# MLP up-projection in seven block products, two pairs interleaved, and the down-projection behind it

## The chip, the cores and the metric

The kernel runs on one core of one Trainium2 chip. The metric is the device time of one execution in microseconds (us). The core has five instruction streams that run beside each other: TensorE (PE, matmuls; its weight loads are listed as PEld), VectorE (DVE), ScalarE (ACT), GpSimd (POOL) and SyncE (SP, which only issues DMAs here). They wait for each other through semaphores.

## The reference, cut to what matters

One encoder layer over 1024 tokens of width 1024. The change concerns the second sub-layer, the gated MLP (`D_FF` = 2816 = 22 x 128), and the output projection `w_o` just ahead of it:

```python
y = _token_mixer(h, ...)          # ends in the product with w_o
x = x + gt1 * _rmsnorm(y, norm_w[l, 1])
h = _rmsnorm(x, norm_w[l, 2]) * (1.0 + sc2) + sh2
...
hu = _dwconv(h @ w_up, conv_w, FFN_CONV // 2) + conv_b     # 1024 -> 5632, width-3 conv over tokens
a, b = jnp.split(hu, 2, axis=-1)
y = (jax.nn.silu(a) * b) @ w_down                           # 2816 -> 1024
x = x + gt2 * _rmsnorm(y, norm_w[l, 3])
```

## The kernel before

Every large product is made three times over: each float32 operand is split by `split` (L166 and L169) into a high part, rounded by ACT, and a low part, the difference, made by DVE or POOL; `mm3` then issues high x high, high x low and low x high into one PSUM bank. One such matmul is 128x512 (128 rows of output, 512 columns).

The last third of the kernel has three stages. (1) `wo_tile(t)` (L1403 on), once for each of eight blocks of 128 tokens: 48 matmuls `y<-wo,mg` into two PSUM banks, k = 0 to 6 of both halves first and k = 7 of both behind, since the merged operand `mg` is ready last for k = 7; then squares on ACT, a power on POOL, scaling and the residual on DVE, and a second norm that leaves `x1[t]`. `h2_half` (L1438) transposes `x1` on PE (`x1T`, eight groups of four), scales it (`hf`) and splits it into `h`. (2) The up-projection, `up_mm`: 44 blocks of 128 rows of `w_up`, each 2 halves x 8 k x 3 = 48 matmuls `hu`, in all 2112. `up` reads the PSUM tile (L1509 on ACT, L1510 and L1511 on DVE: the conv over tokens); `pair(f)` takes block f and block 22+f, applies Silu, multiplies (L1520) and splits the product into `gh`, `gl` in SBUF. (3) The down-projection `down(c)`: two f at a time, 8 token blocks x 2 halves x 2 f x 3 = 96 matmuls `yp`, whose PSUM result DVE adds into `yac` (L1552); in all 1056 matmuls. Stages 2 and 3 alternate: after four pairs, one `down` and two pairs, nine times; `last_down` takes the last four f and ends in the norm and the output.

The weights come by DMA from SP: 512 KB a block (`wur<-w_up`, `wdr<-w_dn`). PSUM has eight banks of 512 columns: `hu` has two tiles of two banks, `yp` four of one bank. The order of instructions on each engine is fixed when the kernel is built, by a scheduler that starts from program order and the dependencies; `T.kept = True` keeps PE's in program order, and the wrapper `InOrder(tc, V)` does so for another engine.

Of the kernel before, what the change touches and what calls it, by code (L numbers as in the profile page):

```python
# [1604 lines left out]
```

## Time and profile before

| | us |
|---|---|
| median of 3 runs | 2046.57 (2046.24 to 2051.73) |
| profiled execution, its own time | 2046.33 |
| span of that execution in the trace | 2044.5 |
| PE busy | 1987.2 (97% of the span) |
| DVE busy | 1198.8 (59%) |
| ACT busy | 776.7 (38%) |
| POOL busy | 318.8 (16%) |
| mean granted PE clock | 0.993 of full speed |

The busy time of PE is read with care: matmuls are pipelined, so the record of one (some 390 ns) overlaps the next. What counts is the spacing from start to start. The chain of waits gives it: a piece of the chain lists a duration and a count of matmuls that ran without waiting. The rows of all views stand in the section of rows, ahead of the prediction.

### The profile page before, as it was taken

How to read it: one execution, taken by the hardware profiler on the slowest of the kernel's cores; microseconds unless marked ns; L12 is line 12 of the kernel's file. 1: busy time of each engine (PE TensorE's matmuls, PEld its weight loads, DVE VectorE, ACT ScalarE, POOL GpSimd, SP SyncE). 2: the span in 40 equal slices, each digit the busy share in tenths (PEclk: the TensorE clock that was granted, in tenths of full speed). 3: DMA queues.
4: the chain of work that ended last, by engine and by line, in shares of the span. 5: the costliest groups of instructions: out<-in, count | busy, mean ns of one | idle time of the engine just before them, and what ended most of it. 6: DMA issues, size and time to landing. Idle time of an engine off the chain costs nothing. (4 is left out here: it accounts for less than half of the span.)

```text
span 2044.5 us, 27253 instructions
## 1 busy us (share of the span) xinstructions
PE 1987.2 (97%) x10846; PEld 1661.5 (81%) x10846; DVE 1198.8 (59%) x2033; ACT 776.7 (38%) x1320; POOL 318.8 (16%) x291
## 2 busy tenths in 40 slices
PE   7999999999999998989999999999999999999998
PEld 6978887888888887768888878878888888888886
DVE  7367867476666658674578653552534454444437
ACT  6464543353353232553555442433221222221222
POOL 4321121141041110133000041010110001000101
PEclk9999999999999999999999999999999999999999
DMA  8321121132121076545201153121111111111113
GB/s 293 114 73 62 43 73 58 47 104 70 34 98 63 31 253 204 162 145 162 90 11 41 43 185 109 69 73 52 42 52 52 52 32 61 52 41 45 48 51 135
DMA packets 68178, 175.09 MB, mean 86 GB/s; under 512 B 10257, under 2 KB 17745, under 8 KB 68050
## 3 DMA queue, kind: packets, MB, share of 16 engines
q1 hardware_dynamic: 54658, 143.13, 22.4%
q10 hardware_dynamic: 11088, 21.83, 2.8%
q0 software_dynamic: 2304, 8.39, 1.0%
q8 instruction: 85, 1.39, 0.3%
q14 instruction: 43, 0.35, 0.1%
HBM read 143.07 MB, written 30.24 MB: 85 GB/s over the span
## 5 line engine op out<-in xcount | busy, mean ns | idle before, releaser
L128 PE MATMUL hu<-h,wuh 128*128 128x512 f32 x1408 | 434.2, 390 | 1.6 <-DVE cv L1511 1.6
L128 PEld LDWEIGHTS hu<-h,wuh 128*128 128x128 f32 x1408 | 263.8, 188 | 56.5 <-ACT cv L1509 2.0
L128 PE MATMUL pj<-hhi,wth 128*128 128x512 f32 x704 | 293.8, 417 | 7.0 <-ACT vN L906 5.4
L128 PE MATMUL pj<-hhi,wtl 128*128 128x512 f32 x704 | 277.3, 394 | 0.0
L128 PE MATMUL pj<-hlo,wth 128*128 128x512 f32 x704 | 275.9, 392 | 0.0
L128 PE MATMUL hu<-h,wul 128*128 128x512 f32 x704 | 274.0, 389 | 0.0
L169 DVE TENSOR_TENSOR wul<-wur,wuh 128x512 fp32r<-128x512 f32 x44 | 30.5, 692 | 215.1 <-ACT wuh L166 215.1
L128 PEld LDWEIGHTS pj<-hhi,wth 128*128 128x128 f32 x704 | 133.5, 190 | 27.9 <-ACT vN L906 5.9
L128 PEld LDWEIGHTS pj<-hhi,wtl 128*128 128x128 f32 x704 | 132.7, 189 | 28.7
L128 PEld LDWEIGHTS hu<-h,wul 128*128 128x128 f32 x704 | 132.2, 188 | 27.5
L169 POOL TENSOR_TENSOR wul<-wur,wuh 128x512 fp32r<-128x512 f32 x44 | 57.6, 1310 | 612.3 <-ACT wuh L166 535.9
L128 PEld LDWEIGHTS pj<-hlo,wth 128*128 128x128 f32 x704 | 133.7, 190 | 20.1
L128 PE MATMUL yp<-wdh,gh 128*128 128x512 f32 x336 | 132.7, 395 | 0.0
L128 PE MATMUL yp<-wdh,gl 128*128 128x512 f32 x336 | 132.7, 395 | 0.0
L128 PE MATMUL yp<-wdl,gh 128*128 128x512 f32 x336 | 132.6, 395 | 0.0
L169 POOL TENSOR_TENSOR wtl<-wtr,wth 128x512 fp32r<-128x512 f32 x44 | 62.3, 1415 | 409.2 <-ACT wth L166 324.3
L166 ACT CAST wuh<-wur 128x512 fp32r<-128x512 f32 x88 | 53.9, 614 | 188.6 <-PE hu L128 188.6
L1552 DVE TENSOR_TENSOR yac<-yac,yp 128x512 f32<-128x512 f32 x128 | 87.1, 686 | 53.5 <-PE yp L128 53.0
L128 PE MATMUL y<-wo,mg 128*128 128x512 f32 x384 | 88.9, 391 | 0.0
L166 ACT CAST wth<-wtr 128x512 fp32r<-128x512 f32 x88 | 53.3, 617 | 83.4 <-PE pj L128 56.2
L128 PEld LDWEIGHTS y<-wo,mg 128*128 128x128 f32 x384 | 71.6, 188 | 15.1 <-DVE mg L169 0.4
L166 ACT CAST wdh<-wdr 128x1024 fp32r<-128x1024 f32 x21 | 22.0, 1049 | 159.4 <-PE yp L128 110.5
(442 smaller groups left out, 4088.7 us busy)
## 6 DMA issues: line engine op xcount, KB each, us to landing
wtr<-w_t SPq DMA_DIRECT2D x44, 512.0 KB, 3.5
wur<-w_up SPq DMA_DIRECT2D x44, 512.0 KB, 3.6
adaw<-w_adaT SPq DMA_DIRECT2D x64, 256.0 KB, 4.0
...
g<-gt_d SPq DMA_DIRECT2D x24, 512.0 KB, 4.3
wdr<-w_dn SPq DMA_DIRECT2D x22, 512.0 KB, 3.6
ada_w<-w_adaT SPq DMA_DIRECT2D x16, 512.0 KB, 5.5
...
```

Source lines behind the costliest of these rows:

```text
L128: self.queue(self.nc.tensor.matmul(out, w, x, **kw), x, 4 if x.dtype == F32 else 1)
L166: ins = A.copy(hi, src)
L169: (eng or V).tensor_tensor(lo, src, r32(hi), op=ALU.subtract)
L1552: V.tensor_tensor(yac[t][:, sl], yac[t][:, sl], ps, op=ALU.add)
```

## The change

**Up-projection.** The 2x2 block form of the product (output rows: block p and block 22+p; inner dimension: k = 0 to 3 and k = 4 to 7; tokens: first and second 512) is computed with seven products of 128x512 over four k, in place of eight. One product is `prod`: 4 k x 3 = 12 matmuls. The products of a pair are `m1` to `m7`; `uA` and `uB` are two PSUM tiles of two banks for each of two pairs in flight, all eight banks. Between products ACT copies a bank (`A.copy` in `m1`, `m7_copy`) and DVE adds a bank and a copy (`e_add`, and the add in `m5`). The operand sums over tokens are built once, in `F` (`t13`, `t2`, `t4`) and split (`hi` on ACT, `lo` on DVE or POOL) into `B11`, `B21`, `T1` to `T4`, `B22`; the weight sums are built for every pair, by DVE (`sums_32`) and POOL (`sums_14`). For the first two pairs `m7` and `m6` are made in two column parts, 384 and 128, since the last 128 tokens come late; `m1` of these two pairs has one matmul more, which starts the second bank.

**Gated product.** `gated` writes `silu(a) * b` to DRAM (`g_d`, 512 KB a pair) instead of splitting it. **Down-projection.** It comes behind all pairs: for each of two groups of 512 tokens (`gr`), 22 f in turn are loaded (`wdr`, 512 KB, and `gr`, 256 KB), split, and multiplied into all eight banks at once, three matmuls to a bank; the last four f go bank by bank. The count stays 2 x 22 x 8 x 3 = 1056. The adds into `yac` are gone.

**Output projection.** `wo_mm` runs all eight k of half 0, then of half 1. `h2_tile` transposes each token block behind the next block's matmuls instead of four blocks at a time. `big` holds 8 tiles of [128, 4, 512] instead of 32 of [128, 512].

```diff
+    def big_tile(nm):
+        return big.tile([P, 4, 512], F32R, tag="big", name=nm, bufs=8)
...
-        xt = tp.tile([P, D], F32, tag="xt", name="xt", bufs=2)
-        SY.dma_start(xt, I["x"][tk, :])
-        x1[t] = x1p.tile([P, D], F32, tag="x1", name="x1", bufs=6)
-        pss = [ps_mm.tile([P, 512], F32, tag="mm", name="y") for _ in range(2)]
-        for ks in (range(KT - 1), (KT - 1,)):
-            for hf in range(2):
-                sl = slice(hf * 512, hf * 512 + 512)
-                for k in ks:
-                    mm3(pss[hf], mg[hf_][0][k][:, c_], mg[hf_][1][k][:, c_], wo[k][0][:, sl], wo[k][1][:, sl], k == 0, k == KT - 1)
+        xts[t] = tp.tile([P, D], F32, tag="xt", name="xt")
+        SY.dma_start(xts[t], I["x"][t * P : (t + 1) * P, :])
+        wo_ps[t] = [ps_mm.tile([P, 512], F32, tag="mm", name="y") for _ in range(2)]
+        for hf in range(2):
+            sl = slice(hf * 512, hf * 512 + 512)
+            for k in range(KT):
+                mm3(wo_ps[t][hf], mg[hf_][0][k][:, c_], mg[hf_][1][k][:, c_], wo[k][0][:, sl], wo[k][1][:, sl], k == 0, k == KT - 1)
...
+    def sums_32(p, eng=V):
+        if p >= NF:
+            return
+        r1, r2 = raws[p]
+        W[p]["s32"] = s32 = wus.tile([P, KT, P], F32, tag="s32", name="s32", bufs=2)
+        p3, p2 = s32[:, 0:4, :], s32[:, 4:8, :]
+        eng.tensor_tensor(p3, r1[:, 0:4, :], r2[:, 0:4, :], op=ALU.add)
+        eng.tensor_tensor(p2, p3, r2[:, 4:8, :], op=ALU.add)
...
+    def split_32(p, copy=A.copy, eng=V):
+        if p >= NF:
+            return
+        s32 = W[p]["s32"]
+        o = [wus.tile([P, KT, P], F32R, tag="wu32", name=f"wu32{m}", bufs=4) for m in "hl"]
+        copy(o[0], s32)
+        yield
+        eng.tensor_tensor(o[1], s32, r32(o[0]), op=ALU.subtract)
+        W[p]["P3"], W[p]["P2"] = ([x[:, n * 4 : n * 4 + 4, :] for x in o] for n in range(2))
...
+    def sums_14(p):
+        if p >= NF:
+            return
+        r1, r2 = raws.pop(p)
+        s14 = wuq.tile([P, KT, P], F32, tag="s14", name="s14")
+        G.tensor_tensor(s14[:, 0:4, :], r2[:, 0:4, :], r2[:, 4:8, :], op=ALU.add)
+        G.tensor_tensor(s14[:, 4:8, :], r1[:, 4:8, :], W[p].pop("s32")[:, 4:8, :], op=ALU.add)
+        for nm, src, n, eng in (("P1", s14[:, 0:4, :], 4, G), ("A22", r2[:, 4:8, :], 4, V), ("P4", s14[:, 4:8, :], 2, G)):
+            W[p][nm] = [wuq.tile([P, 4, P], F32R, tag="wu" + nm, name=f"wu{nm}{m}", bufs=n) for m in "hl"]
+            split(W[p][nm][0], W[p][nm][1], src, eng)
+    def prod(ps, w, x, start, cols=slice(0, 512)):
+        for k in range(4):
+            wh, wl, xh, xl = w[0][:, k, :], w[1][:, k, :], x[0][:, k, cols], x[1][:, k, cols]
+            T.matmul(ps[:, cols], wh, xh, start=start and k == 0, stop=False, skip_group_check=True)
+            T.matmul(ps[:, cols], wh, xl, start=False, stop=False, skip_group_check=True)
+            T.matmul(ps[:, cols], wl, xh, start=False, stop=k == 3, skip_group_check=True)
...
+    def t13(c):
+        pV.tensor_tensor(blk(0, 0, c), blk(0, 0, c), blk(1, 0, c), op=ALU.subtract)
+        pV.tensor_tensor(blk(1, 0, c), blk(1, 1, c), blk(1, 0, c), op=ALU.subtract)
+    def t2(c):
+        pV.scalar_tensor_tensor(blk(1, 0, c), blk(0, 0, c), -1.0, blk(1, 1, c), op0=ALU.mult, op1=ALU.subtract)
+    def t4(c):
+        pV.scalar_tensor_tensor(blk(0, 1, c), blk(1, 0, c), -1.0, blk(0, 1, c), op0=ALU.mult, op1=ALU.subtract)
+    def hi(nm, c):
+        pA.copy(X[nm][0][:, :, c], blk(*home[nm], c))
+    def lo(nm, c, eng=pV):
+        eng.tensor_tensor(X[nm][1][:, :, c], blk(*home[nm], c), r32(X[nm][0][:, :, c]), op=ALU.subtract)
...
+    def m1(p, A=A):
+        a, b = uA[p % 2][:, half[1]], uA[p % 2][:, half[0]]
+        if p < 2:
+            T.matmul(b, W[p]["A11"][0][:, 0, :], X["B11"][0][:, 0, :], start=True, stop=True, skip_group_check=True)
+        prod(a, W[p]["A11"], X["B11"], True)
+        A.copy(b, a)
+    def m2(p):
+        prod(uA[p % 2][:, half[0]], W[p]["A12"], X["B21"], False)
+    def m7_part(p, cols):
+        prod(uB[p % 2][:, half[0]], W[p]["P3"], X["T3"], cols.start == 0, cols)
+    def m7_copy(p):
+        m7s[p] = tg.tile([P, 512], F32, tag="m7", name="m7", bufs=2)
+        A.copy(m7s[p], uB[p % 2][:, half[0]])
+    def m7(p):
+        if p < NF:
+            m7_part(p, slice(0, 512))
+            m7_copy(p)
+    def m6_part(p, cols):
+        prod(uA[p % 2][:, half[1]], W[p]["P2"], X["T2"], False, cols)
+    def e_add(p):
+        V.tensor_tensor(uB[p % 2][:, half[0]], uA[p % 2][:, half[1]], m7s[p], op=ALU.add)
+    def m6(p):
+        m6_part(p, slice(0, 512))
+        e_add(p)
+    def m5(p):
+        a, d = uA[p % 2][:, half[1]], uB[p % 2][:, half[1]]
+        prod(a, W[p]["P1"], X["T1"], False)
+        V.tensor_tensor(d, a, m7s.pop(p), op=ALU.add)
+    def m3(p):
+        prod(uB[p % 2][:, half[0]], W[p]["A22"], X["T4"], False)
+    def m4(p):
+        prod(uA[p % 2][:, half[1]], W[p]["P4"], X["B22"], False)
...
+    sums_32(0, pV)
+    next(norm)
+    hi("T3", c0)
+    m1(0, pA)
+    m2(0)
+    sums_32(1, G)
+    sp = [split_32(0, pA.copy, pV), split_32(1, pA.copy, G)]
+    next(sp[0])
+    lo("T3", c0)
+    next(norm)
+    next(norm)
+    hi("B22", c0)
+    next(sp[0])
+    next(norm)
+    next(sp[1])
+    next(sp[1])
+    lo("B22", c0, G)
+    m1(1, pA)
+    m2(1)
+    hi("T1", c0)
+    t2(c0)
+    h2_tile(KT - 1, [uB[1][:, half[0]], uB[1][:, half[1]]], pV, pA)
+    hi("T2", c0)
+    lo("T2", c0)
+    lo("T1", c0, G)
+    t13(c1)
+    hi("T3", c1)
+    lo("T3", c1)
+    hi("B22", c1)
+    lo("B22", c1, G)
+    hi("T1", c1)
+    lo("T1", c1, G)
+    t2(c1)
+    hi("T2", c1)
+    lo("T2", c1)
+    for p in range(2):
+        m7_part(p, c0)
+    for p in range(2):
+        m6_part(p, c0)
+    for c in parts:
+        t4(c)
+        hi("T4", c)
+        lo("T4", c)
...
+    def gated(p):
+        a = conv(p, uA[p % 2])
+        A.activation(a, a, AF.Silu)
+        V.tensor_tensor(a, a, cb.pop(p), op=ALU.mult)
+        A.dma_start(g_d[p], a)
...
+    m5(0)
+    sums_14(1)
+    m5(1)
+    m3(0)
+    second_row(0)
+    m4(0)
+    gated(0)
...
+    for p in range(2, NF):
+        m6(p)
+        m7(p + 1)
+        m2(p)
+        m5(p)
+        m1(p + 1)
+        m3(p)
+        second_row(p)
+        m4(p)
+        sums_14(p + 1)
+        gated(p)
+        up_load(p + 2)
+        sums_32(p + 2)
+        drain(split_32(p + 2))
...
+    def down_step(gr, f):
+        graw = dw.tile([P, 512], F32, tag="gr", name="gr", bufs=4)
+        raw = down_raw(gr, f, graw)
+        wd = [dw.tile([P, D], F32R, tag=f"wd{m}", name=f"wd{m}", bufs=6) for m in "hl"]
+        gg_ = [dw.tile([P, 512], F32R, tag=f"g{m}", name=f"g{m}", bufs=6) for m in "hl"]
+        split(gg_[0], gg_[1], graw)
+        split(wd[0], wd[1], raw, G if f % 3 == 2 else V)
+        steps[gr, f] = wd, gg_
+    def down_mm(gr, f, t, hf):
+        wd, g = steps[gr, f]
+        tk = slice(t * P, (t + 1) * P)
+        mm3(ys[t][hf], g[0][:, tk], g[1][:, tk], wd[0][:, half[hf]], wd[1][:, half[hf]], f == 0, f == NF - 1)
...
+        for f in range(f0, LAST):
+            for t in range(4):
                 for hf in range(2):
...
+                    down_mm(gr, f, t, hf)
+            get(1)
+        for t in range(4):
+            c = {}
+            for hf in range(2):
+                for f in range(LAST, NF):
+                    down_mm(gr, f, t, hf)
+                finish(gr, t, hf, c)
+            if gr == 0:
```

How the order of ACT changes where the first products begin: first the kernel before, at the end of the second `h2_half` (`hf` are 128x512 groups of `x1T`, `h` their splits; `wuh` and `wdh` are weights, `cv` the first conv).

```order
L166 CAST h_13102<-hf_13184 128x512
L1447 ACTIVATE hf_13196<-x1T,sh_7567,sm_7566 128x512
L166 CAST h_13103<-hf_13196 128x512
L166 CAST wdh<-wdr 128x1024
L166 CAST h_13104<-hf_13211 128x512
L166 CAST wuh<-wur 128x512
L1509 ACTIVATE cv<-hu,fcb,fcw 128x1024
```

Then the change, from the norm of the last token block on (`x_13077` is that block, `F_12390` and `F_12391` the two token halves, `COPY uA` the copy in `m1` of pairs 0 and 1, `wu32h` the weight sums of the two pairs).

```order
L103 ACTIVATE x_13077,s_13078<-y 128x512 x2
L1468 ACTIVATE F_12391<-x1T,sh_7567,sm_7566 128x128 x4
L103 CAST T3h<-F_12391 128x4x384
L103 COPY uA<-uA 128x512
L103 CAST wu32h<-s_13109 128x1024
L103 ACTIVATE x_13077,s_13078<-xt 128x1024
L103 CAST B22h<-F_12391 128x4x384
L103 CAST wu32h<-s_13146 128x1024
L103 COPY uA<-uA 128x512
L103 CAST T1h<-F_12390 128x4x384
L103 ACTIVATE F_12391<-uB,sh_7567,sm_7566 128x128 x4
L103 CAST T2h<-F_12391 128x4x384
```

The casts of `h` between the matmuls are replaced by a fixed row in which the copies of `uA`, for which PE's next product waits, stand behind casts of whole operand sums.

DVE in the steady part: the last adds of a `down` and one pair of the kernel before.

```order
L1552 TENSOR_TENSOR yac_13252<-yac_13252,yp 128x512 x2
L169 TENSOR_TENSOR wdl<-wdr,wdh 128x1024 x2
L169 TENSOR_TENSOR wul<-wur,wuh 128x512
L1510 SCALAR_TENSOR_TENSOR cv<-hu,fcw,cv 128x1023
L1511 SCALAR_TENSOR_TENSOR cv<-hu,fcw,cv 128x1023
L169 TENSOR_TENSOR wul<-wur,wuh 128x512
L1510 SCALAR_TENSOR_TENSOR cv<-hu,fcw,cv 128x1023
L1511 SCALAR_TENSOR_TENSOR cv<-hu,fcw,cv 128x1023
L1520 TENSOR_TENSOR cv<-cv 128x1024
L169 TENSOR_TENSOR gl<-cv,gh 128x1024
```

The same engine in the change, one pair from `m3` on (`wuA22l` is the weight of the next pair, `L1709` and `L1710` the conv, `L1622` `e_add`, `L1631` the add in `m5`).

```order
L169 TENSOR_TENSOR wuA22l<-wur,wuA22h 128x512
L1709 SCALAR_TENSOR_TENSOR cv<-uB,fcw,cv 128x1023
L1710 SCALAR_TENSOR_TENSOR cv<-uB,fcw,cv 128x1023
L1709 SCALAR_TENSOR_TENSOR cv<-uA,fcw,cv 128x1023
L1622 TENSOR_TENSOR uB<-uA,m_14606 128x512
L1710 SCALAR_TENSOR_TENSOR cv<-uA,fcw,cv 128x1023
L1516 TENSOR_TENSOR wu32l<-s_14834,wu32h 128x1024
L1721 TENSOR_TENSOR cv<-cv 128x1024
L1506 TENSOR_TENSOR s_14964<-wur 128x512
L1507 TENSOR_TENSOR s_14964<-s_14964,wur 128x512
L169 TENSOR_TENSOR wu1l<-wur,wu1h 128x1024
L1631 TENSOR_TENSOR uB<-uA,m_14606 128x512
```

The splits of `gl` and the adds into `yac` are gone from the row, and sums, two adds on PSUM and a wider low part of the weights stand in it.

## Rows read from the trace of the kernel before

**Rows 1.** The page's busy times, share of the span and instructions of each engine.

```profile
PE 1987.2 (97%) x10846; PEld 1661.5 (81%) x10846; DVE 1198.8 (59%) x2033; ACT 776.7 (38%) x1320; POOL 318.8 (16%) x291
```

**Rows 2.** Windows: stretch, length; PE, PEld, DVE, ACT, POOL busy; clock; DMA.

```profile
1208.00:1332.00 124.00, 121.79 (x565) 100.01 (x565) 60.49 (x100) 46.76 (x90) 22.37 (x29) 1.00 0.29 103
1332.00:1990.80 658.80, 658.80 (x2881) 540.75 (x2882) 294.53 (x316) 167.81 (x203) 53.70 (x41) 1.00 0.17 50
```

**Rows 3.** Chain that ended last, from `wo` on: start, duration, engine, tile, line.

```profile
1213.16 64.87 PE y L128 x285
...
1317.18 0.44 PE x1T L131 x4
...
1397.50 22.39 PE yp L128 x96
1419.89 43.53 PE hu L128 x192
...
1990.84 41.71 PE yp L128 x180
...
2040.52 0.66 DVEq L1601
```

**Rows 4.** PE's waits from 1200 us on: sum, times, longest.

```profile
PE hu L128 <- DVE cv L1511: 1.6, 1, 1.6
```

**Rows 5.** Timeline at the start of `wo`: start, duration, work, idle before.

```profile
1213.00 11.30 PE L128 MATMUL y<-wo,mg 128*128 128x512 f32 x48
...
1220.08 1.17 ACT L166 CAST mg<-g 128x512 fp32r<-128x512 f32 x2 [2.69 <-DVE g L1392]
1220.73 1.29 DVE L169 TENSOR_TENSOR mg<-g,mg 128x512 fp32r<-128x512 f32 x2
```

**Rows 6.** Instructions by form, 1332 to 1990 us: count, busy us, mean ns.

```profile
L1511 DVE SCALAR_TENSOR_TENSOR cv<-hu,fcw,cv 128x1023 f32<-128x1023 f32 x42 | 53.8, 1281 | 1.2
...
L169 POOL TENSOR_TENSOR wul<-wur,wuh 128x512 fp32r<-128x512 f32 x41 | 53.7, 1310 | 587.9 <-ACT wuh L166 511.5 <-DVE yac L1552 76.4
L166 ACT CAST wuh<-wur 128x512 fp32r<-128x512 f32 x82 | 50.3, 613 | 186.1 <-PE hu L128 186.1
L1509 ACT ACTIVATE cv<-hu,fcb,fcw 128x1024 f32<-128x1024 f32 x41 | 49.3, 1203 | 0.0
L169 DVE TENSOR_TENSOR wul<-wur,wuh 128x512 fp32r<-128x512 f32 x41 | 28.4, 692 | 210.8 <-ACT wuh L166 210.8
...
L169 DVE TENSOR_TENSOR gl<-cv,gh 128x1024 fp32r<-128x1024 f32 x21 | 25.7, 1226 | 15.1 <-ACT gh L166 15.1
...
L166 ACT CAST gh<-cv 128x1024 fp32r<-128x1024 f32 x21 | 22.1, 1051 | 79.0 <-DVE cv L1520 79.0
```

**Rows 7.** The same by form, 1205 to 1340 us.

```profile
L1430 DVE SCALAR_TENSOR_TENSOR x<-y,s,gt1w 128x512 f32<-128x512 f32 x16 | 11.3, 747 | 5.0 <-POOL s L1427 5.0
...
L1449 DVE TENSOR_SCALAR hf<-x1T,sm,sh 128x512 f32<-128x512 f32 x8 | 6.5, 807 | 1.5 <-PE x1T L131 1.4
...
L1447 ACT ACTIVATE hf<-x1T,sh,sm 128x512 f32<-128x512 f32 x8 | 6.2, 776 | 5.5 <-DVE h L169 3.3 <-PE x1T L131 2.2
L1436 DVE TENSOR_SCALAR x<-xt,s 128x1024 f32<-128x1024 f32 x8 | 6.0, 753 | 5.5 <-POOL s L1435 5.5
```

**Rows 8.** Timeline of DVE and of POOL, where both work, and an undisturbed one.

```profile
1334.74 1.21 DVE L169 TENSOR_TENSOR wdl<-wdr,wdh 128x1024 fp32r<-128x1024 f32 x1
1335.87 2.31 DVE L1520 TENSOR_TENSOR cv<-cv 128x1024 f32<-128x1024 f32 x1
...
1358.23 1.23 DVE L1520 TENSOR_TENSOR cv<-cv 128x1024 f32<-128x1024 f32 x1
...
1335.18 1.92 POOL L169 TENSOR_TENSOR wul<-wur,wuh 128x512 fp32r<-128x512 f32 x1 [4.15 <-ACT wuh L166]
```

**Rows 9.** A long wait of PE earlier in the kernel, and the window behind it.

```profile
788.93 0.80 PE L128 MATMUL pj<-hhi,wth 128*128 128x512 f32 x1 [5.44 <-ACT vN L906]
789.52 0.63 PE L128 MATMUL pj<-hlo,wth 128*128 128x512 f32 x1
...
789.00:794.00 5.00, 5.00 (x12) 3.95 (x13) 3.48 (x12) 1.11 (x2) 2.01 (x1) 0.50 0.85 270
```

**Rows 10.** The page's DMA issues: count, KB each, median us to landing.

```profile
wur<-w_up SPq DMA_DIRECT2D x44, 512.0 KB, 3.6
...
g<-gt_d SPq DMA_DIRECT2D x24, 512.0 KB, 4.3
```

More of the change, by code (lines that the diff above doesn't have):

```diff
@@ L1481, in build @@
-    steps = lambda it, n: [next(it) for _ in range(n)]
-    steps(ua, KT)
-    steps(ub, 3)
-    steps(tr, 3)
-    steps(ub, KT - 3)
-    for k in range(KT):
-        steps(tr, int(k < KT - 3))
-        steps(ua, 1)
-        steps(ub, int(k > 2))
-    drain(tr)
-    T.kept = False
+    ps_u = pool(psE, "ps_u", space=PSUM)
+    uA = [ps_u.tile([P, S], F32, tag=f"uA{n}", name="uA") for n in range(2)]
+    uB = [ps_u.tile([P, S], F32, tag=f"uB{n}", name="uB") for n in range(2)]
+    half = (slice(0, 512), slice(512, S))
@@ new lines, in build @@
+    next(norm)
+    next(sp[1])
[21 more added lines that the diff above has]
+        m7_part(p, c0)
+    for p in range(2):
+        m6_part(p, c0)
@@ new lines, in build, with second_row @@
+    cb = {}
+    def second_row(p):
+        cb[p] = conv(NF + p, uB[p % 2])
+    def gated(p):
[3 more added lines that the diff above has]
+        A.dma_start(g_d[p], a)
+    for p in range(2):
+        m7_part(p, parts[1])
+        m7_copy(p)
+    sums_14(0)
+    for p in range(2):
+        m6_part(p, parts[1])
+        e_add(p)
+    m5(0)
[5 more added lines that the diff above has]
+    gated(0)
@@ new lines, in build @@
+    up_load(2)
+    sums_32(2)
+    drain(split_32(2))
+    m3(1)
+    second_row(1)
+    m7(2)
+    sums_14(2)
+    m4(1)
+    gated(1)
+    m1(2)
+    up_load(3)
+    sums_32(3)
+    drain(split_32(3))
+    for p in range(2, NF):
[12 more added lines that the diff above has]
+        drain(split_32(p + 2))
+    steps = {}
@@ new lines, in build @@
+    EARLY = 5
+    early_steps(EARLY)
+    ffE.close()
+    hxE.close()
+    psE.close()
+    psE = ExitStack()
+    ps_y = pool(psE, "ps_y", space=PSUM)
+    banks = [ps_y.tile([P, 512], F32, tag=f"y{n}", name="y") for n in range(8)]
+    ys = [[banks[n], banks[n + 1]] for n in (0, 4, 6, 2)]
+    dnE = ExitStack()
+    dw = pool(dnE, "dw", side="right")
+    def down_step(gr, f):
[6 more added lines that the diff above has]
+        steps[gr, f] = wd, gg_
@@ new lines, in build, with get @@
+    LAST = NF - 4
+    order = [(gr, f) for gr in range(2) for f in range(NF)]
+    ahead = iter(order[EARLY:])
+    def get(n):
+        for _ in range(n):
+            if (o := next(ahead, None)) is not None:
+                down_step(*o)
+    for gr in range(2):
+        f0 = 0
+        if gr == 0:
+            for ts in ((0, 1), (2, 3)):
+                for f in range(3):
+                    for t in ts:
+                        for hf in range(2):
+                            down_mm(gr, f, t, hf)
+                    if ts[0] == 0:
+                        get(1)
+            f0 = 3
+        for f in range(f0, LAST):
+            for t in range(4):
+                for hf in range(2):
+                    down_mm(gr, f, t, hf)
+            get(1)
+        for t in range(4):
+            c = {}
+            for hf in range(2):
+                for f in range(LAST, NF):
+                    down_mm(gr, f, t, hf)
+                finish(gr, t, hf, c)
+            if gr == 0:
+                get(1)
@@ L1587, in build @@
+    T.kept = False
+    dnE.close()
     wuE.close()
```

269 lines of the change are left out of this document (143 added, 126 removed).

## The prediction

> **What bounds the kernel now.** I read the busy times first [rows 1]: PE works 97% of the span, DVE 59%. From 1332.0 to 1990.8 us, where the up- and down-projections alternate, PE is busy 658.80 of 658.80 us at full clock [rows 2], and the chain that ended last is one piece of PE after another [rows 3]. So the MLP lasts as long as its matmuls: a saved matmul is worth its spacing, a new wait its whole length. The spacings are 43.53/192 = 0.2267 us for `hu`, 22.39/96 = 0.2332 for `yp`, 64.87/285 = 0.2276 for `y`, and 0.44/4 = 0.11 for a transpose [rows 3]. The three differ in how often the PSUM bank changes: every 24 matmuls in `hu`, every 6 in `yp`, every 12 on the average in `y` (runs of 21 and of 3).
>
> PE's path of before, from its first `y` at 1213.0 [rows 5]: 384 x 0.2276 = 87.4, 64 transposes 7.0, 2112 x 0.2267 = 478.8, 1056 x 0.2332 = 246.2, waits of some 2.3 (the longest 1.6 [rows 4]): PE ends near 2035. The tail to the span's end is some 9.3 us, and the execution's own time lies 1.8 us above its span (2046.33 against 2044.5). That execution is 0.2 us from the median, so its sum stands for the median.
>
> **The matmuls.** 22 pairs x 7 products x 12 = 1848 take the place of 2112. 1800 of them are whole. Products change bank every 12 matmuls, as `y` does on the average, so I take 0.2276: 409.7 us; at `hu`'s 0.2267 it would be 408.1. The first two pairs' `m7` and `m6` are 48 matmuls cut into 384 and 128 columns: 0.17 by proportion and something between 0.057 (a quarter) and 0.11 (a transpose has 128 columns), 0.253 together, 12.1 us. Two extra matmuls cost 0.45. The products take 422.3 us where `hu` took 478.8.
>
> The down-projection keeps 1056 matmuls but changes bank every 3. If the 0.0065 us between `hu` and `yp` comes with the bank change, one change costs 0.052 us and runs of 3 give 0.2419; `y` fits a smaller price, and if the bank plays no part 0.2332 stays. No row has runs of 3 alone; I take 0.237, or 250.3 us, with 246.2 and 255.4 as ends. PE's work from 1213.0 is then 87.4 + 7.0 + 422.3 + 250.3 = 767.0 us, without waits up to 1980.0.
>
> **The start of `wo`.** Half 0 now comes to k = 7 after 21 matmuls, at 1217.8, but its high part is cast at 1220.08 and its low part made at 1220.73 [rows 5], where a first op of each pair takes about 0.6. Before, 42 matmuls lay ahead. New wait 3.2 us.
>
> **The ramp.** Count from T = 0, where the seventh token block's transposes begin. `m1(0)` ends at 3.8. `m2(0)` needs the copy of `uA`, which ACT makes only behind the cast `T3h`, and that waits for DVE's `t13` behind ACT's scaling of the block (2.75). The ops have 1536 columns: by the slope of 692 and 1226 ns for 512 and 1024 columns, 1.77 us each on DVE; by 613 and 1051, 1.49 on ACT [rows 6]. So 2.75 + 2 x 1.77 + 1.49 + 0.61 = 8.4: a wait of 4.6 us. In the same way: `m2(1)` waits 1.6 (its copy stands behind a square, `B22h` and `wu32h` on ACT). `m5(0)` waits longest: DVE and ACT take turns over `t2`, the scaling of the last block (0.4 for 128 columns, from 807 and 776 for 512 [rows 7]), `T2l`, the 128-column part, `t4` and `T4l`, which ends at 35.7; only then may POOL begin `sums_14` in the same buffers, and sum, cast, sum and `P1l` (3 x 1.31 + 0.61, [rows 6]) end at 39.6 or 39.7. PE has its parts of `m7` and `m6` done at 32.7: 6.8 us with both halves of the wait. `m5(1)` waits 2.5 for the next four POOL ops, `m7(2)` 1.0, `m6(2)` 1.6, one part of `m6` 0.4. Sum 18.5 us. Durations are used where the spacing of ops back to back is some 0.07 less (1.21 at 1334.74, next start 1335.87 [rows 8]); over some 24 DVE ops in a row this gives back 1.7.
>
> **DVE against POOL.** At 1335.18 POOL starts a 512-column subtraction while DVE is in `wdl` until 1335.95; POOL takes 1.92 where its mean is 1.31. DVE then starts `L1520` at 1335.87 and takes 2.31, not 1.23, ending 1.1 us behind POOL's end [rows 8]: they ran one after the other. In the ramp POOL has `B22l` and `T1l` (three times 1.31 each), `wu32l` of pair 1 (2.6) and two small parts, 13.1 us, beside DVE ops with two SBUF inputs. Taking whichever is ready first, DVE's `T4l` ends at 42.3, not 35.7: 6.6 us more on `m5(0)`. Ends: 0, and 13.1 if all of it is in line. The Trainium skill ("SBUF — State Buffer", section "SBUF: two separate sides") says that a GpSimd op and a VectorE op with two SBUF inputs hold one shared port pair in turn, each for its whole length, and this speaks against a change that gives POOL more to do. By it every such meeting costs, and the sum stands; if the one collision in [rows 8] were an accident, the sum would be 6.6 lower.
>
> **The clock.** After the wait of 5.44 us at 788.93 the window 789 to 794 has 12 matmuls in 5.00 us and a granted clock of 0.50 [rows 9], against 22 at full clock: 2.3 us lost. After the 1.6 of [rows 4] the clock stayed at 1.00 [rows 2]. The ramp has one wait of over 5 us and several of 2 to 5: I take 3 us, ends 0 and 7.
>
> **The steady part.** PE per pair: 84 x 0.2276 = 19.1 us. DVE: 4 conv ops at 1.28, four 1024-column ops at 1.23, five of 512 columns at 0.69 = 13.5 at most; ACT 8.6; POOL 4 x 1.31 = 5.2 [rows 6]. PE stays the bound. The tightest hand-over: `m7` of the pair after next writes the bank that the conv reads. From the end of `m3`: `A22h` 0.61, conv on ACT 1.20, two on DVE 2.56, hand-overs, about 4.7; PE has `m4` and `m6`, 24 x 0.2276 = 5.46, in between. Slack 0.7; I count no wait. `m2` and `m3` have 1.4 to 2 in hand. POOL's four ops fall 0.6 to 5.9 us after `m4`, where DVE's ops read PSUM; only `wu32l` meets one, 0.6 us, ahead of an add with 2 us in hand. SP's loads land in 3.6 us [rows 10] and are issued a pair ahead. If this cover goes, each us is paid 20 times.
>
> **Between and in the down-projection.** The last conv ends some 3 us before PE needs the banks, and g of the last pair is read only 11 us after its store. In the loop a step moves 768 KB in 24 x 0.237 = 5.7 us, 135 GB/s, where [rows 9] show 270 GB/s moved; landing 4.3 for 512 KB [rows 10] is hidden by steps loaded ahead. ACT has 1.7 and DVE 1.9 in those 5.7 us. The adds into `yac` and the splits of `gl`, `gh` lay beside PE: nothing gained. The change of token group costs some 1 us. The tail exchanges one add (0.69) for an add of the residual: nothing.
>
> **Sum.** 1980.0 + 3.2 + 18.5 - 1.7 + 6.6 + 3 + 1 = 2010.6 for PE's end, + 9.3 + 1.8 = 2021.7. I forecast 2022, 1.2% faster; own range 2012 to 2032.
>
> **Rivals.** (A) The ramp costs less: no collisions (-6.6), clock kept (-3), spacings of `hu` and `yp` (-5.7): 2006. For it: the waits are chains of estimates. Against it: [rows 8]. (B) The spacing at the upper end (+5.1) and 0.3 to 0.5 us of wait in each of 20 pairs (+6 to +10), from the slack of 0.7 being less than counted: 2033 to 2037, up to 2040 with more ramp; PE's idle share before [rows 2] does not tell, since `hu` had two tiles to alternate. (C) Slower: the hand-over from `m3` to `m7` becomes late by w in each pair and the clock falls behind it each time: 20 x (w + 2.3); at w = 0.5 this is 56 us, 2078. Without the clock it decides from w = 1.5 on (20 x 1.5 = 30), which needs 2.2 us more in a chain of 4.7, two POOL ops ahead of `wuA22l`. For it: [rows 9]; against it: the 1.6 of [rows 4] left the clock at 1.00. (D) That fewer matmuls don't come out: the order shows 1848 and 2 for the products, so this has no chance.
>
> **How the numbers follow.** 0.3% is about what a measurement of this kernel can tell. Forecast (2012 to 2032) 0.52; A (1998 to 2012) 0.17, still less 0.04; B (2032 to 2040) 0.10; between (2040 to 2053) 0.07; C 0.10. Faster 0.83, same 0.07, slower 0.10. The range 2000 to 2042 leaves out C, the upper part of the middle and the ends of A.
>
> **What would show it.** In the changed trace: PE's waits at `y` (3 us), `uA` ahead of `m2` (4.6 and 1.6) and of `m5` (some 13 and 2.5), and next to none from the third pair on; pairs 19.1 us apart; 24 down matmuls in 5.6 to 5.8 us; POOL ops of 1.9 us or more in the ramp; PE's end near 2010. The forecast is wrong if pairs are 20 us or more apart, or if PE shows half clock outside the ramp.

## The result, and the profile after

The changed kernel takes 2021.56 us (median of 4 runs, 2019.83 to 2023.77) against 2046.40 before: a ratio of 0.9873, 95% interval 0.9853 to 0.9893. The forecast was 2022. The profiled execution took 2022.97 us, with a span of 2020.8.

The page's busy times after, beside [rows 1]: PE works 46 us less, DVE 52 and POOL 117 us more.

```profile
PE 1941.0 (96%) x10632; PEld 1622.5 (80%) x10632; DVE 1251.0 (62%) x2049; ACT 858.3 (42%) x1440; POOL 436.1 (22%) x364
```

The windows below cut the MLP's part after into `wo`, the ramp, the loop over pairs and the down-projection (columns as in [rows 2]). The first one opens at 1214.50, 2.4 us behind the first `y` matmul (1212.09).

```profile
1214.50:1309.46 94.96, 92.35 (x425) 76.17 (x424) 46.28 (x87) 35.19 (x82) 21.12 (x28) 0.98 0.27 100
1309.46:1383.70 74.24, 55.85 (x260) 44.99 (x258) 62.29 (x59) 36.71 (x51) 37.07 (x22) 0.91 0.18 59
1383.70:1769.16 385.46, 382.69 (x1657) 311.66 (x1658) 241.29 (x231) 161.33 (x199) 101.34 (x80) 1.00 0.26 88
1769.16:2012.90 243.74, 241.06 (x1056) 198.96 (x1055) 91.05 (x113) 73.81 (x111) 35.95 (x20) 0.99 0.48 152
```

Before, PE was busy in every one of 658.80 us [rows 2]. After, it is idle 18.4 us of the ramp, and some 2.7 us in each of the other stages. From the first `y` matmul to the span's end it was 831.5 us before and is 808.7 now. This length is what I compare below: the stages ahead of it do the same work in all kernels but their end moves between 1208.0 and 1215.6 us from profile to profile, so a median carries a few us that no edit made.

PE's waits after (sum, times, longest), where before had one of 1.6 [rows 4]:

```profile
PE uA L128 <- ACT wuP1h L166: 5.6, 1, 5.6
PE uA L128 <- ACT uA L103: 4.7, 2, 4.0
PE uA L128 <- ACT uA L1601: 4.4, 1, 4.4
PE y L128 <- DVE yo L1832: 2.7, 1, 2.7
PE y L128 <- ACT mg L166: 2.6, 1, 2.6
PE uA L128 <- POOL wuP1l L169: 1.7, 2, 1.1
...
PE uA L128 <- DVE uB L1622: 1.5, 1, 1.5
PE uB L128 <- DVE uB L1631: 1.2, 1, 1.2
```

The first is `m5` of the first pair, the second `m2` of the first two pairs, the third `m6` of the third pair (all ramp), the fourth the change of token group, the fifth the start of `wo`; the last two are the last pair of the loop. Between the third pair and the last one no wait is listed.

One period of the loop in the chain that ended last (start, duration, tile, matmuls): `m4` and `m6`, then `m7`, then `m2`, `m5` and `m1`, then `m3`, 84 matmuls in 19.28 us.

```profile
1440.51 5.51 PE uA L128 x24
1446.02 2.72 PE uB L128 x12
1448.74 8.25 PE uA L128 x36
1456.99 2.80 PE uB L128 x12
```

`m7` has 2.72/12 = 0.2267 us a matmul and `m3` 2.80/12 = 0.2333, though both are 12 matmuls into one bank of `uB`. Stage by stage, forecast and measured (us; "rest" is the tail to the span's end):

| | `wo` | ramp | loop | down | rest | sum |
|---|---|---|---|---|---|---|
| forecast | 95.9 | 73.5 | 376.9 | 251.3 | 9.3 | 806.9 |
| measured | 97.2 | 74.25 | 385.45 | 243.95 | 7.9 | 808.7 |

The sum is 1.8 off, but the loop is 8.6 longer and the down-projection 7.4 shorter than forecast. These two errors were the first thing to explain.

### The profile page after: what moved, and what is told of

It reads as the page before. It is cut to its first block, busy times and chain, and to the rows that moved or that the text cites. A ratio compares the mean times of both kernels' runs of the same rounds, so it can differ in the third digit from the quotient of the medians.

```text
span 2020.8 us, 27349 instructions
## 1 busy us (share of the span) xinstructions
PE 1941.0 (96%) x10632; PEld 1622.5 (80%) x10632; DVE 1251.0 (62%) x2049; ACT 858.3 (42%) x1440; POOL 436.1 (22%) x364
## 3 DMA queue, kind: packets, MB, share of 16 engines
q8 instruction: 83, 1.36, 0.3%
## 5 line engine op out<-in xcount | busy, mean ns | idle before, releaser
L128 PE MATMUL y<-wdh,gh 128*128 128x512 f32 x312 | 122.2, 392 | 2.7 <-DVE yo L1832 2.7
L128 PE MATMUL y<-wdl,gh 128*128 128x512 f32 x312 | 122.1, 391 | 0.0
L128 PE MATMUL y<-wdh,gl 128*128 128x512 f32 x312 | 121.9, 391 | 0.0
L169 DVE TENSOR_TENSOR gl<-gr,gh 128x512 fp32r<-128x512 f32 x39 | 30.2, 781 | 113.1 <-ACT gh L166 113.1
L169 POOL TENSOR_TENSOR wuP4l<-s,wuP4h 128x512 fp32r<-128x512 f32 x22 | 30.0, 1365 | 273.4 <-ACT wuP4h L166 273.4
L579 ACT CAST tU<-pu 128x512 f16<-128x512 f32 x80 | 44.2, 587 | 94.1 <-PE pu L128 93.5
L573 DVE TENSOR_TENSOR pm<-pp,msk 128x512 f16<-128x512 f32 x96 | 63.4, 685 | 15.7 <-PE pp L128 15.0
L169 DVE TENSOR_TENSOR wuA22l<-wur,wuA22h 128x512 fp32r<-128x512 f32 x22 | 18.4, 840 | 87.3 <-ACT wuA22h L166 86.1
L584 DVE CAST tT<-pq 128x512 f16<-128x512 f32 x96 | 62.7, 684 | 15.4 <-PE pq L128 15.1
L128 PEld LDWEIGHTS y<-wdh,gh 128*128 128x128 f32 x312 | 58.9, 189 | 15.5 <-DVE yo L1832 3.1
L128 PEld LDWEIGHTS y<-wdh,gl 128*128 128x128 f32 x312 | 59.0, 189 | 12.4
```

Source lines behind the costliest of these rows:

```text
L128: self.queue(self.nc.tensor.matmul(out, w, x, **kw), x, 4 if x.dtype == F32 else 1)
L169: (eng or V).tensor_tensor(lo, src, r32(hi), op=ALU.subtract)
L573: V.tensor_tensor(pm, v4(pp), b4(msk[:, l, 1 - d, :]), op=ALU.mult)
L579: A.copy(nU, v4(pu))
L584: V.tensor_copy(nT, v4(pq))
```

## Experiments

Ratios are to the kernel before, with 95% intervals; stage lengths come from the profiled execution of each. Such a length is one reading: where two kernels have the same code in a stage, the loop still reads 384.8 to 386.4 us and the down-projection 242.4 to 245.2, mostly since the granted clock falls behind a wait in one profile and not in another. Differences of that size in a stage that an edit leaves alone are not put down to the edit.

**What sets the spacing.** Rival theories: (bank) every change of the PSUM bank costs, as I had predicted; (place) the two operands' places in SBUF decide. As the kernel after lays its tiles out, the weights `P1`, `A22` and `P4` of `m5`, `m3` and `m4` start 96 bytes past a multiple of 256 and their moving operands 128 past; in the other products both lie at 128. These three have the longer spacing. Widening one small tile by 32 bytes moves the three weights to 128:

```
-    fcb = tg.tile([P, 44], F32, tag="fcb", name="fcb")
-    SY.dma_start(fcb, I["f_cb"])
+    fcb = tg.tile([P, 52], F32, tag="fcb", name="fcb")
+    SY.dma_start(fcb[:, 0:44], I["f_cb"])
```

> One edit: the tile ahead of the pool of the weights P1, A22, P4 is 32 bytes longer, so that these weights begin at the same place within 256 bytes as the moving operands do (both 128; in the changed kernel 96 against 128). Theory 1, the spacing of a matmul depends on where its two operands lie relative to each other: m3, m4, m5 go from 0.2335 to 0.2267 us, a pair from 19.28 to 19.04, 22 pairs x 36 x 0.0067 = 5.3 us less than the changed kernel, some 2016. Theory 2 (the prediction's), the spacing comes with the change of PSUM bank: no change, 2021.5.

The same with 84 in place of 52 puts them at 0, against 128:

> The same tile is 160 bytes longer: the weights begin at a multiple of 64 bytes, but 128 bytes apart from the moving operand within 256 (0 against 128), as gh and wd did in the kernel before. If only the alignment of the weights to 64 bytes counts, m3, m4, m5 take 0.2267 and the time falls by 5.3 us as in al32; if the relative place counts, they stay at 0.2333 and so does the time, some 2021; by the bank theory also 2021.

The kernel before has such matmuls too, `yp`, with `wd` at 0 against 128; there the same is done with the tile `s3`:

```
-                s2 = tp.tile([P, 2], F32, tag="s3", name="s3", bufs=4)
+                s2 = tp.tile([P, 10], F32, tag="s3", name="s3", bufs=4)
```

> The kernel before with one edit: a small tile is 128 bytes longer in all, so that wd begins at the same place within 256 bytes as gh (128 and 128; before 0 and 128). Relative-place theory: yp goes from 0.2332 to 0.2267 us, 9 x 96 + 144 = 1008 matmuls x 0.0066 = 6.6 us less than before, some 2039.8. Bank theory: no change, 2046.5.

The chain of the first, from `m7` on:

```profile
1442.16 2.72 PE uB L128 x12
1444.88 8.16 PE uA L128 x36
1453.04 2.72 PE uB L128 x12
1455.76 5.44 PE uA L128 x24
```

`m3` of the second:

```profile
1440.92 2.79 PE uB L128 x12
```

And of the third, beside the 22.39 and 43.53 of [rows 3]:

```profile
1397.59 21.76 PE yp L128 x96
1419.35 43.52 PE hu L128 x192
```

With equal places all products run at 0.2267 (2.72, 8.16, 5.44), and the MLP's part is 802.9 us, 5.8 less than after; the median is 2013.60 (0.984, 0.9824 to 0.9857). The loop has 4.4 of this, where 5.3 were expected for all 22 pairs. Another 1.6 lies in the down-projection, which the edit leaves as it is: behind its wait of 2.7 us the clock stays at full in this profile (15 matmuls in 3.40 us, against 8 in after).

```profile
1887.60:1891.00 3.40, 3.40 (x15) 2.78 (x16) 3.40 (x5) 1.57 (x2) 1.48 (x1) 1.00 0.99 391
```

At 0 against 128, 2.79/12 = 0.2325 and nothing is gained (808.5; 2021.91, 0.988, 0.9863 to 0.9898), so it is not that the weights lie on a round address. In the kernel before, `yp` falls from 0.2332 to 0.2267 and the part from 831.5 to 825.0 (2041.08, 0.9974, 0.9962 to 0.9986), with its banks changing as often as ever. The bank theory fell: banks change every 3 matmuls in the down-projection of after, and 1039 of its 1055 spacings lie below 0.231; both operands start at 0 there, or both at 128. Three pairs of places were tried (equal, 32 apart, 128 apart); what in the engine does this stays open.

**VectorE against GpSimd.** In the ramp VectorE's scaling of a block takes 3.97 us where the same form took 0.753 before [rows 7]. Timeline of VectorE, then of GpSimd, after:

```profile
1323.44 3.97 DVE L103 TENSOR_SCALAR x<-xt,s 128x1024 f32<-128x1024 f32 x1 [0.46 <-POOL s L1452]
1327.33 3.95 DVE L103 SCALAR_TENSOR_TENSOR F<-F,F 128x1536 f32<-128x1536 f32 x1
...
1333.36 2.89 DVE L103 TENSOR_TENSOR T2l<-F,T2h 128x1536 fp32r<-128x1536 f32 x1
```

```profile
1323.38 3.47 POOL L1580 TENSOR_TENSOR B22l<-F,B22h 128x1536 fp32r<-128x1536 f32 x1
1326.82 2.84 POOL L1516 TENSOR_TENSOR wu32l<-s,wu32h 128x1024 fp32r<-128x1024 f32 x1
1329.62 5.01 POOL L1580 TENSOR_TENSOR T1l<-F,T1h 128x1536 fp32r<-128x1536 f32 x1
```

The experiment gives VectorE what GpSimd does there:

```
-    sp = [split_32(0, pA.copy, pV), split_32(1, pA.copy, G)]
+    sp = [split_32(0, pA.copy, pV), split_32(1, pA.copy, pV)]
...
-    lo("B22", c0, G)
...
-    lo("T1", c0, G)
+    lo("T1", c0)
...
-    lo("B22", c1, G)
...
-    lo("T1", c1, G)
+    lo("T1", c1)
...
         hi("T4", c)
+        lo("B22", c)
         lo("T4", c)
```

> The changed kernel with the four big low parts that POOL makes in the ramp (B22l, wu32l of pair 1, T1l, and the 128-column parts; some 13 us on POOL) made by DVE instead, B22l behind T4h. Theory of turns (an op of POOL and an op of DVE on SBUF run one after the other): DVE's row of single ops gets 6.2 us longer in work but loses collisions of 3.2, 2.2, 1.1 and 1.0 us and more, T4l ends 1 to 2 us earlier than in the changed kernel, m5(0) likewise, time -1 to -2 us. If they did not take turns, T4l would end 2 to 5 us later and so would the kernel.

Its VectorE in the same stretch:

```profile
1323.28 0.75 DVE L103 TENSOR_SCALAR x<-xt,s 128x1024 f32<-128x1024 f32 x1 [0.46 <-POOL s L1452]
...
1325.08 1.75 DVE L103 SCALAR_TENSOR_TENSOR F<-F,F 128x1536 f32<-128x1536 f32 x1
...
1333.65 1.75 DVE L103 TENSOR_TENSOR T2l<-F,T2h 128x1536 fp32r<-128x1536 f32 x1
```

3.97 becomes 0.75, 3.95 and 2.89 become 1.75: that the two engines hold each other up is shown, and a VectorE op with one SBUF input is held up too. This is what the Trainium skill states ("SBUF — State Buffer", section "SBUF: two separate sides"): a GpSimd op and a VectorE op that has two SBUF inputs or runs in a two-port mode hold one port pair in turn, for the whole instruction. No run here shows whether the scaling ran in such a mode. But the time didn't come back: ramp 74.3 (74.25), part 809.0 (808.7), median 2021.08 (0.9872, 0.9852 to 0.9892), where 1 to 2 us were expected. VectorE has the work itself now, and its `T4l`, on which the first pair's sums wait, ends 0.6 us later behind the last `wo` matmul than in after.

**Is one wait of the ramp worth its length?** `m2` of the first pair waits 4.0 us because ScalarE copies `uA` behind the cast `T3h`. Swapped:

```
-    hi("T3", c0)
     m1(0, pA)
+    hi("T3", c0)
```

> The changed kernel with one pair of lines in the ramp in the other order: the copy of uA in m1(0) stands ahead of the cast T3h on ACT. Additive theory (the prediction counts each wait in full): the wait of 4.0 us of m2(0) goes, 4 to 6 us less, some 2016.5. Chain theory: the ramp ends when DVE and POOL have made T4l and then P1l; PE comes earlier to m2(0) and waits as much longer at the later places, m5(0) begins at the same time, 0 to 1 us less, 2021.

PE's waits in its ramp and behind it:

```profile
PE uA L128 <- ACT wuP1h L166: 5.6, 1, 5.6
...
PE uA L128 <- ACT uA L103: 1.3, 2, 0.7
```

The 4.0 is gone (0.66 is left of it; the next product, `m1` of the second pair, now waits 1.9) and next to nothing is gained: ramp 73.9 for 74.25, median 2021.79 (0.9873, 0.9851 to 0.9895). The part is 807.4, 1.3 less than after, mostly by the down-projection (1.6 shorter, again with no half clock behind its wait), not by the ramp. The first `m5` waits the same 5.6 us. It waits for a chain on ScalarE and VectorE that begins with `T3h` and ends with `T4l`, behind which GpSimd makes its sums. ScalarE's `T3h` and GpSimd's first sum in after, then in the experiment:

```profile
1315.29 1.47 ACT L103 CAST T3h<-F 128x1536 fp32r<-128x1536 f32 x1 [3.70 <-DVE F L103]
...
1349.50 1.26 POOL L1526 TENSOR_TENSOR s<-wur 128x512 f32<-128x512 f32 x1 [7.63 <-issue]
```

```profile
1317.71 1.49 ACT L103 CAST T3h<-F 128x1536 fp32r<-128x1536 f32 x1 [1.38 <-DVE F L103]
...
1351.84 1.26 POOL L1526 TENSOR_TENSOR s<-wur 128x512 f32<-128x512 f32 x1 [7.63 <-issue]
```

The last `wo` matmul ended at 1309.30 in after and at 1311.72 here, so `T3h` starts 5.99 us behind it in both, and the sum 40.2 and 40.1 us behind it. ("issue" is the row's guess; `T4l` ends 0.1 us before the sum starts, at 1349.37, and in the experiment with VectorE above the row names it.) PE's 4.0 lay beside this chain, not on it; PE's waits in the ramp are no list of separate prices.

**The slack of the hand-over from `m3` to `m7`.** Each of 18 pairs (those from the third to the twentieth) gets one or two superfluous copies on ScalarE ahead of the conv's first op, each some 1.0 us:

```
-    def conv(f, ps):
+    def conv(f, ps, extra=0):
         o = tg.tile([P, S], F32, tag="cv", name="cv", bufs=3)
+        for _ in range(extra):
+            A.copy(o, ps)
...
-        cb[p] = conv(NF + p, uB[p % 2])
+        cb[p] = conv(NF + p, uB[p % 2], 1 if 2 <= p < NF - 2 else 0)
```

> The changed kernel with one useless copy of uB by ACT (about 1.1 us) ahead of the conv of the second row in pairs 2 to 19, so that the hand-over from m3 to m7 is 1.1 us longer. The trace of the changed kernel has the conv's last op end 1.2 us ahead of m7, where the prediction counted 0.7. With 1.2 of slack: no change, 2021.5, no wait of PE in the steady part. With 0.7: 18 x 0.4 = 7 us more.

> The same with two copies, 2.2 us: m7 of 18 pairs waits some 1.0 us each. Rival C of the prediction (the clock falls behind each wait): 18 x (1.0 + 2.3) = 59 us, some 2080. Forecast's view (a wait of this length leaves the clock alone): 18 x 1.0, some 2040, granted clock 1.00 in the steady part.

In after, the conv's last op of one pair ends at 1425.39 and the `m7` behind it starts at 1426.6, 1.2 us later; 0.14 of this is the hand-over itself, as the chain with two copies shows (1468.13 to 1468.27). With one copy the loop grows by 3.7 us (389.2; part 812.4; median of two runs 2029.66, 8.1 above after's, 0.9911, 0.9886 to 0.9936). At `m7` no wait is listed, but in each of the 18 pairs its first matmul is followed after 0.27 to 0.31 us instead of 0.2267, as behind a wait: the copy has used the slack up, and this makes 1.4. Some 2.1 lie at `m3`. Its waits in the loop, and the chain ahead of one of them:

```profile
PE uB L128 <- DVE uB L1631: 2.4, 4, 1.1
```

```profile
1488.96 5.18 DMA wur<-w_up
...
1497.83 0.62 DVE uB L1631
...
1498.50 3.06 PE uB L128 x12
```

Three of these four are new (the last pair's is in after too). `m3` waits for an add on VectorE that stands behind the sums of a freshly loaded block, and the load waits for GpSimd's sums to free the buffer. So a second chain was nearly as tight. With two copies, PE's longest list entry and the clock of a window in the loop are:

```profile
PE uB L128 <- DVE cv L1712: 16.4, 19, 0.9
```

```profile
1400.00:1700.00 300.00, 285.92 (x1228) 228.84 (x1227) 170.21 (x175) 150.24 (x179) 76.24 (x60) 1.00 0.23 78
```

Now every pair pays: loop 407.0, 21.6 more than after; median 2045.90 (0.9996, 0.9984 to 1.0007), the whole gain gone. 18 of the 19 waits lie in the loop. The list counts a wait from the modelled end of the matmul before, 0.39 us after its start, where the next one usually starts after 0.2267. From start to start a pair loses more than the listed 0.9: 1.06 ahead of `m7`'s first matmul (1.29 for 0.2267, at 1466.98), and 0.08 behind it (0.31 for 0.2267). 18 such pairs make 20.5 of the 21.6. The clock stays at 1.00, so these waits didn't drop it.

**Start of `wo`.** The first token block takes its k-blocks 0 to 6 of both halves first, and the block that comes late behind them:

```
-        for hf in range(2):
+        for hf, k in [(h, k) for ks in ((range(KT - 1), (KT - 1,)) if t == 0 else (range(KT),)) for h in range(2) for k in ks]:
...
-            for k in range(KT):
+            if True:
```

> The changed kernel with the old order of k in the first token block of the output projection alone (k = 0 to 6 of both halves, then k = 7). Theory: the wait of 2.6 us at the start goes, and with it the half clock behind it (six matmuls at 0.43 instead of 0.23, 1.2 us): 3.8 us less than the changed kernel, some 2017.7. Rival: the ramp is set by chains that begin at the end of the projection and simply move with it, so that all of it is gained; if they hung on something earlier (loads of weights), less than 1.5 us.

The chain at this place in after begins its unbroken run of `y` at 1219.85, behind the wait. With the new order:

```profile
1208.61 22.02 PE y L128 x96
```

The wait of 2.6 us is gone, and with it the half clock behind it: `wo` 92.8 (97.2), part 805.2, median 2017.02 (0.9853, 0.9837 to 0.9869). Of the 4.4 us of this stage 3.5 are left in the part; the loop is 1.0 longer in this profile (386.4), as 13 matmuls run at half clock behind the third pair's `m6`, where after has 8.

**Change of token group.** GpSimd has every third split of the down weights, and I took the power op for the norm to stand in its queue behind one. All splits to VectorE:

```
-        split(wd[0], wd[1], raw, G if f % 3 == 2 else V)
+        split(wd[0], wd[1], raw)
```

> The changed kernel with all low parts of the down weights made by DVE, none by POOL. Theory: the wait of 2.7 us at the change of token group is the power on POOL standing behind a 2.4 us subtraction there, and half clock behind it costs some 1.5 us more: both go, 4 us less than the changed kernel, some 2017.5. Rival: another chain (ACT's casts of the next steps ahead of the squares) ends as late, and less than 1.5 us is gained.

GpSimd, VectorE, and GpSimd again in after:

```profile
1888.39 2.42 POOL L169 TENSOR_TENSOR wdl<-wdr,wdh 128x1024 fp32r<-128x1024 f32 x1 [3.25 <-ACT wdh L166]
1888.91 2.44 DVE L169 TENSOR_TENSOR gl<-gr,gh 128x512 fp32r<-128x512 f32 x1 [0.52 <-ACT gh L166]
...
1893.30 1.46 POOL L1830 TENSOR_TENSOR s<-s,mhalf 128x1 f32<-128x1 f32 x1 [2.50 <-DVE s L1829]
```

The power op (L1830) does not stand behind the split: GpSimd is idle for 2.50 us before it and waits for VectorE. VectorE is late, since its split `gl` takes 2.44 us beside GpSimd's; in the experiment it takes 0.69. PE's wait falls from 2.7 to 1.5, with no half clock behind it: down-projection 241.2 (243.95). Of these 2.7 us 1.2 are the wait; the 1.6 of half clock are not shown to be the edit's: of the nine profiles of changed kernels without it, two have none there either. The loop is 1.0 longer in this profile, so the part is 807.0, 1.7 less; the median, 2017.96 (0.9859, 0.9844 to 0.9873), is 3.6 less, and 4 were expected.

**Sums in place.** The sums for `P1` and `P4` go into the load buffers, so that they need no free tile:

```
-        s14 = wuq.tile([P, KT, P], F32, tag="s14", name="s14")
-        G.tensor_tensor(s14[:, 0:4, :], r2[:, 0:4, :], r2[:, 4:8, :], op=ALU.add)
-        G.tensor_tensor(s14[:, 4:8, :], r1[:, 4:8, :], W[p].pop("s32")[:, 4:8, :], op=ALU.add)
+        G.tensor_tensor(r2[:, 0:4, :], r2[:, 0:4, :], r2[:, 4:8, :], op=ALU.add)
+        G.tensor_tensor(r1[:, 4:8, :], r1[:, 4:8, :], W[p].pop("s32")[:, 4:8, :], op=ALU.add)
...
+        for nm, src, n, eng in (("P1", r2[:, 0:4, :], 4, G), ("A22", r2[:, 4:8, :], 4, V), ("P4", r1[:, 4:8, :], 4, G)):
```

> The changed kernel with the sums for P1 and P4 made in place in the loaded weights instead of in a tile of their own, and twice the buffers for P4 (same memory). The tile of its own lies where F lies, so POOL's sums for pair 0 stood behind T4l; in place they can be made before the ramp. Chain theory: m5(0) begins one sum (1.3 us) earlier, m5(1) up to 3 us earlier, and m4(1), m6(2), whose weights waited for m4(0) to free P4, some 2 to 4 us earlier; 3 to 6 us less in all, 2016 to 2018.5. Rival: the waits are DVE's and ACT's own, and the gain is given back at the next place (m6 of pair 2 waits for DVE): under 1.5 us.

Its GpSimd where the last norm begins:

```profile
1311.95 3.01 POOL L1525 TENSOR_TENSOR wur<-wur 128x512 f32<-128x512 f32 x2 [8.21 <-DVE s L103]
1314.92 0.55 POOL L1443 TENSOR_TENSOR s<-s,mhalf 128x1 f32<-128x1 f32 x1
```

The first `m5` waits 4.7, 0.9 less than in after, but it starts later: 44.1 us behind the last `wo` matmul (which ended at 1305.37), where after has 42.2. The sums are made early, as meant, but the norm's power op (L1443) now stands behind two of them, 9.6 us behind that matmul instead of 7.6, and `T4l` ends at 42.9 instead of 40.1. So work was taken from the end of the chain and put in at its start. A later product waits 1.7 where after has 0.5: the chain of waits there runs through the next pairs' loads (3.65 us of `wur` at 1351.47), into buffers that are now held longer. Ramp 74.6, part 809.2, median 2022.56 (0.9875, 0.986 to 0.989): no gain.

**Together.** First the shifted weights with the last three edits, then without the sums in place:

> All that helped or should: the changed kernel with the 32 bytes of al32, the low parts of dvw, the order of k7 and the sums of ip. If the gains add up (7.9, 3.5, 3.8, 4): some 2002 to 2004. If the ramp gives back what the start gains: 2006 to 2008.

> The changed kernel with the 32 bytes of al32, the low parts of dvw and the order of k7, without the in-place sums of ip. The three gains lie in three stages (pair loop 7.9, down-projection 3.5, start of the output projection 4.5) and none of them sets another's chain, so they should add: some 2006, range 2003 to 2009. If ip's sums were worth something in company of the others, this is no better than best1's 2011.5.

The first has a part of 801.1 us (median 2011.52, 0.9823, 0.9808 to 0.9837), the second 797.6 (2010.81, 0.9823, 0.981 to 0.9837). The medians don't tell them apart; by stages the sums in place cost 3.5, all in the loop (384.7 against 381.3). The second is 11.1 below after in its MLP part. In the stages that the three edits touch, they alone gave 4.4 (loop), 4.4 (`wo`) and 2.7 us (down-projection), and together 4.2, 4.4 and 2.8, so they add up. Its median was expected at 2003 to 2009 and missed that by 2 us. It is 10.75 us below after and the fastest version found.

## Why the prediction was right, point by point

That the total came out within 2 us is in part luck: the loop was forecast 8.6 us too short and the down-projection 7.4 too long, and the two nearly cancel.

**PE bounds, and a saved matmul is worth its spacing.** Right. 264 matmuls fewer (before: 2112 at 0.2267) and 48 smaller ones gave the gain, and in the loop PE is busy 382.69 of 385.46 us.

**Spacing by bank changes.** Wrong, the step that failed. The three spacings of before [rows 3] fitted the bank, but the edit to the kernel before shows that `yp` had its spacing from its operands' places. This mis-sized two terms in opposite directions. The products: 0.2276 taken for all, measured 0.2267 where the places are equal and some 0.233 where they are not, in 36 matmuls of each pair; these lose 4.7 us over 0.2267 in the loop, where I had 1.5. The down-projection: 0.237 taken, 0.2267 measured, so 1056 x 0.0103 = 10.9 us less than the 250.3. I named 246.2 as the lower end of that term; 1056 x 0.2267 = 239.4 lies below it, and 24 matmuls take 5.44 us, not the 5.6 to 5.8 that I gave as a sign. `yp` at 0.2332 was taken as a floor with no reason.

**The loop's 8.6 us.** Against 376.9: the products at 0.233 take 3.2 more; the two waits at the last pair, listed as 1.5 and 1.2, take 3.3 from start to start, where I had none; and half clock behind the late `m6` of the ramp, 8 matmuls in 3.40 us where 1.81 is usual (a row below), 1.6. That makes 8.1; the rest lies in single spacings. Why the last pair waits, ScalarE's timeline of after shows: its conv stands in the queue behind casts of the down-projection, which wait for their loads.

```profile
1747.54 2.00 ACT L166 CAST wd<-wdr 128x1024 fp32r<-128x1024 f32 x2
1749.44 1.20 ACT L1708 ACTIVATE cv<-uB,fcb,fcw 128x1024 f32<-128x1024 f32 x1
1752.01 0.62 ACT L166 CAST gg<-gr 128x512 fp32r<-128x512 f32 x1 [1.36 <-DMA gr<-g_d]
...
1753.05 1.20 ACT L1708 ACTIVATE cv<-uA,fcb,fcw 128x1024 f32<-128x1024 f32 x1
```

The 1.36 for the load and the 2.00 for the casts are about what the two waits take; that is argued from these rows, not tried.

**Start of `wo`.** 3.2 us forecast, 2.6 measured, plus 1.2 of half clock that I had put to the ramp alone.

**The ramp's 18.5 us of waits.** The length was right (73.5 against 74.25), the list only in part. `m2` 4.6 and 1.6 forecast, 4.0 and 0.7 measured. `m5` some 13 with the collisions and 2.5; measured 5.6 with 0.6 behind it, and 1.1: `T4l` ended 40.1 us after the last `wo` matmul (forecast 42.3), and PE had its parts of `m7` and `m6` done at 36.6, not 32.7. `m6` of the third pair 1.6, measured 4.4, with the clock halved behind it. A wait of 1.6 at the last block's transposes was not on my list. The 48 matmuls cut in two took 0.173 and 0.111, 0.284 together for my 0.253, 1.5 us in all. (My 39.6 for `P1l` is 35.7 and three GpSimd ops; with the cast that I named beside them it would be 40.2.) As the swapped copy showed, the waits ahead of `m5` don't add to the ramp: the chain to `T4l` sets it.

**VectorE against GpSimd, 6.6 us.** The mechanism is right and its rows stronger than I had (three ops, 10.81 where 4.25 would do, by the experiment's 0.75 and twice 1.75). Its price in the ramp was not: taken away, it gives nothing measurable, since moving the work costs as much. At the change of token group, where I had not looked for it, taking it away shortened PE's wait by 1.2. In the loop `wu32l` takes 1.911 us in the mean of 18, 0.7 more than the form's usual, and hides, as forecast.

**The clock, 3 us.** Low. In after five stretches ran at half clock, 1.2 GHz, one behind each wait of 2.6 us and more (here the first four; the fifth, behind the change of token group, has 8 matmuls in 3.40 us as well):

```profile
1219.85:1222.00 2.15, 2.15 (x5) 1.72 (x6) 1.27 (x2) 0.96 (x2) 0.00 (x0) 0.50 0.15 63
1317.30:1322.00 4.70, 4.70 (x11) 3.73 (x12) 4.52 (x6) 2.77 (x4) 0.77 (x3) 0.50 0.09 38
1351.40:1354.00 2.60, 1.94 (x4) 1.12 (x5) 1.96 (x2) 1.68 (x4) 2.60 (x3) 0.50 0.35 66
1383.60:1387.00 3.40, 3.40 (x8) 2.66 (x9) 2.01 (x2) 1.49 (x2) 1.85 (x2) 0.51 0.89 231
```

In them 37 spacings of about 0.43 stand where 0.2267 would: 37 x 0.2 = 7.4 us, just over the term's upper end of 7. Three of the five (22 of the 37) lie outside the ramp, which I had named as a sign that the forecast is wrong: the clock's part of it was. What the clock does behind a given wait is not fixed, though. The wait of 2.7 us at the change of token group left it at 1.00 with the shifted weights (the row in the experiments) and with the swapped copy, and so did a wait of 3.1 us in the latter, while a wait of 1.9 us there was followed by 0.50.

**The steady part.** No wait in the pairs between, as forecast. The slack of `m7` is 1.05 behind the hand-over, not 0.7. "`m2` and `m3` have 1.4 to 2 in hand" was wrong for `m3`: 1.0 of lateness made it wait, by way of GpSimd, a load and VectorE.

**Rivals.** Rival A was right that the down-projection's spacing is lower, and still too high (0.2332, measured 0.2267). Rival C's place is right, and it does decide by lateness in every pair, but its first form (the clock falls each time) is refuted by 18 waits at clock 1.00. Its second form nearly holds: `m7` came late by 1.06 in 18 pairs, and each paid 1.14.

**Tail and the change of group.** 7.9 where 9.3 was kept; 2.7 of wait and 1.6 of half clock where 1 was taken.
